# Weights as one stream, all queues ordered by a timeline simulation, and the first block's waits moved, in a two-layer hybrid decoder trunk

## The chip, the cores and the metric

The kernel runs on one core of a Trainium2 chip. The metric is the device time of one execution in microseconds (us). A core has five engines that run side by side, each with its own queue of instructions in a fixed order: TensorE (PE, matmuls; its weight loads are shown apart as PEld), VectorE (DVE), ScalarE (ACT), GpSimd (POOL) and SyncE (SP), which here only issues DMA transfers. An engine takes its instructions strictly in their order, and each of them waits until what it reads is written and what it overwrites has been read.

## What is computed

The reference is a trunk of `DEPTH` = 2 layers over one sequence of 512 tokens and 1024 channels, in float32. Cut to what matters:

```python
for l in range(DEPTH):
    u = rmsnorm(h, norm_w[l])
    proj = u @ w_in[l]                       # one combined input projection
    ret_p, diff_p, ssd_p, ml_p = split_cols(proj, ...)
    ret_out  = retention_mixer(...) * silu(rz)          # chunks of 128 tokens, a state carried over
    diff_out = diff_attention_mixer(...) * silu(dz)     # softmax(q1 k1) - lam * softmax(q2 k2), causal
    ssd_out  = _rms(ssd_mixer(...) * silu(sz)) * ssd_norm_w[l]   # Mamba-2, causal conv, chunked scan
    ml_out   = mlstm_mixer(...) * silu(mz)              # stabilised mLSTM, causal conv, chunked
    mix = concatenate([ret_out, diff_out, ssd_out, ml_out])      # 2048 wide
    h = h + mix @ w_out[l]
return rmsnorm(h, final_norm_w)
```

## The kernel before, in words

**Precision and tiles.** Each matmul operand is split into a high part and a low part, and each product takes three matmuls: high by high, low by high, high by low. A matmul row in the trace is mostly 128x128 weights against 128x512 data. The input projection has 15 blocks of 512 columns per layer, each 8 slices (`k`) of 128 input channels deep; the output projection has four groups (`r`, `d`, `s`, `m`, one per mixer) of two halves with 4 slices each. The list `ORDER` names the sequence of a layer: mLSTM's blocks first (`mv`, `gates`, `mq`, ...), then those of differential attention, then `m` (the out-projection of mLSTM), the blocks of SSD, `d`, and so on to `r`, which ends the layer. `proj_tok` runs a block with tokens on the output's partitions, `proj_feat` one with features there, `out_proj` an out-projection, which adds its result onto the residual `h` (L657).

**Weights.** `split_w` loads two slices (512 KB) with one DMA on SP's queue (L366) into one of 2 buffers named `raw`; `split_half` then makes for each slice `whi` on ACT (a cast, L357, or L360 with a scale for out-projections) and `wlo` on DVE (a subtraction, L358, or L361 with the scale). There are 10 buffers of `whi` and 10 of `wlo`, so one block of 8 slices and 2 slices of the next fit. A `raw` buffer comes free when both `wlo` made of it are done. `load_block` and `out_proj` issue the 4 loads of a block in the program where its projection begins. The first block of all (`mv` of layer 0) has its weights loaded by `start` in 8 pieces named `z`.

**What sets the order.** TensorE's order is written by a planner in the kernel: the projections form a main line (`filler`), and the mixers are generators that are put into it (`spawn`, `later`, `due`, `drive`) at times which the planner counts by costs in the table `W`. ACT, DVE, POOL and SP are ordered by the framework's scheduler from the program's order and its priorities: in the kernel before by priority, with the splits of weights raised by `high_priority(W["hp"])`, 100. The first block (`start`) is under `manual_schedule` for ACT, DVE, POOL and SP: there the written order counts.

**The first block.** `start` has steps per token tile `t`: `squares(t)` (ACT, L390), `scale(t)` (two small DVE instructions L395 and L397, then a power -0.5 on POOL, L240), `mul(t)` (two DVE instructions L404 that write the normed tile `e`), `trans(t)` (8 transposes on PE, L131, in two banks, then a copy `uh` on ACT, L347, and a subtraction `ul` on DVE, L348). `hi(k)` and `lo(k)` make `whi` and `wlo` of slice `k` (L414, L418). `run(pr[t], n)` lets the projection of tile `t` issue n of its 16 pieces; the string `orders` lists the pieces (`h3` is the two matmuls with `whi` of slice 3, `l3` the one with `wlo`). `setup` also issues matmuls of a tile of ones (`warm`). The small parameter loads (`rows`, `w`, `cv`) are prepared by ACT (L313) and DVE (L304, L314, L295, L298).

**Places that are named later.** L1157 is a DVE copy of a PSUM bank in `diff_av` (differential attention); L544 multiplies a gate into the bank of a projection; L954 is a product in `ssd` that TensorE's next matmuls read; L950 and L995 stand ahead of it; L604 and L606 apply rotary embeddings; L623 makes the low part of a mixer's output for `out_proj`; L253, L257, L260, L240 and L330 are the norm of the next layer (squares on ACT, two small DVE steps, the power on POOL, the product on DVE).

Of the kernel before, what the change touches and what calls it, by code (L numbers as in the profile page):

```python
# [11 lines left out]
F32 = mybir.dt.float32  # L12
# [9 lines left out]
NT = S // P  # L22
# [41 lines left out]
     'sN': 0.0, 'sF': 7.3, 'rC': 2.3, 'rN': 3.0, 'dT': 9.14, 'dN': 1.0, 'dM': 3.0, 'dV': 6.68, 'dF': 14.0,  # L64
     'm0': 6.4, 's0': 8.8, 'dT1': 0.6, 'dN1': 1.0, 'hp': 100, 'he': 100, 'hr': 50, 'hd': 50, 'dS': 4.7, 'dQ': 6.0,
     'ha': 50}
# [33 lines left out]
class Trunk:  # L100
    def __init__(self, ctx, tc, aps, dbg=None):
        self.tc, self.nc = tc, tc.nc
        self.x, self.win, self.wg, self.wout, self.nrm, self.rows, self.convp, self.cst, self.out = aps
        self.dbg = dbg or {}
        mk = lambda n, b, **k: ctx.enter_context(tc.tile_pool(name=n, bufs=b, **k))
        self.cp = mk("cp", 1)


        self.small = mk("small", 1)
        self.hp = mk("hp", 1)  # L110
        self.pool = mk("pool", 1)
# [87 lines left out]
    def setup(self):  # L199
# [151 lines left out]
    def split_half(self, raw, scale):  # L351
        nc = self.nc
        hi = self.t("whi", [P, 512], F32R, bufs=10)
        lo = self.t("wlo", [P, 512], F32R, bufs=10)
        with self.tc.high_priority(W["hp"]):
            if scale is None:
                nc.scalar.copy(out=hi, in_=raw)  # L357
                nc.vector.tensor_tensor(out=lo, in0=raw, in1=hi.bitcast(F32), op=ALU.subtract)  # L358
            else:
                nc.scalar.activation(hi, raw, AF.Copy, scale=scale)  # L360
                nc.vector.scalar_tensor_tensor(lo, raw, scale, hi.bitcast(F32), ALU.mult, ALU.subtract)  # L361
        return hi, lo
# [5 lines left out]

    def load_block(self, name):
        b = BIDX[name]  # L370
        return [q for g in range(4) for q in self.split_w(self.win[self.l, b, :, 2 * g:2 * g + 2, :])]

    def start(self, evac):
# [46 lines left out]
        with self.tc.manual_schedule(engines={E.Activation, E.DVE, E.Pool, E.SP}):  # L420
# [206 lines left out]
    def out_proj(self, g, mixt, tok_outer=False, after=None, cut=False, heads=False):  # L627
        nc = self.nc
        gi = GROUPS[g]
        nw = self.nwc[g]  # L630
        w = [[x for q in range(2) for x in self.split_w(self.wout[self.l, gi, half, :, 2 * q:2 * q + 2, :],
                                                        nw[2 * q:2 * q + 2])]
             for half in range(2)]
        l = self.l
        order = [(t, hf) for t in range(NT) for hf in range(2)] if tok_outer else \
                [(t, hf) for hf in range(2) for t in range(NT)]
        for t, hf in order:
# [5 lines left out]
            for c0, c1 in zip(cuts, cuts[1:]):  # L643
# [5 lines left out]
                for k in range(4):  # L649
                    hi, lo = w[hf][k]  # L650
# [705 lines left out]
```

## Time and profile before

| | |
|---|---|
| median of 3 runs | 1045.69 us (1043.56 to 1046.55) |
| the profiled execution | 1043.91 us, of which the span from first to last instruction is 1042.1 us |
| mean granted TensorE clock | 0.994 |
| PE busy | 1023.0 us (98% of the span), 5110 instructions |
| DVE / ACT / POOL busy | 693.2 us (67%) / 479.7 us (46%) / 164.9 us (16%) |
| DMA | 93.84 MB, mean 90 GB/s; the weights' loads of 512 KB land 3.9 us (w_in) and 3.5 us (w_out) after they are issued |

A row of the trace's timeline has the start, the duration, the engine, the line, the operation with out<-in, the shape and a count; in brackets stands the idle time of the engine before it and what released it. Idle time counts only on the engine that sets the end.

### The profile page before, as it was taken

The numbers are of one execution on the slowest core, as the hardware profiler recorded it, in microseconds if no ns is written. First come the engines' busy times: TensorE is split into PE (matmuls) and PEld (weight loads), VectorE is DVE, ScalarE is ACT, GpSimd is POOL, SyncE is SP. The second block draws the span as 40 slices with busy tenths as digits, with TensorE's granted clock in tenths as the row PEclk, the third lists the DMA queues.
The fourth block names the chain that finished last, engine by engine and source line by source line (L and its number), as shares of the span: only waits on it lengthen the run. The fifth ranks groups of instructions, "written<-read, shape, count | busy, mean of one in ns | idle before, by whom it ended". The sixth has DMA issues, their size and how long they took to land.

```text
span 1042.1 us, 14190 instructions
## 1 busy us (share of the span) xinstructions
PE 1023.0 (98%) x5110; PEld 835.1 (80%) x5110; DVE 693.2 (67%) x1495; ACT 479.7 (46%) x1057; POOL 164.9 (16%) x204
## 2 busy tenths in 40 slices
PE   8999999999999999999999999999999999999997
PEld 6788888877778887878887888887777888878786
DVE  5588675567787867446655967666667786863454
ACT  4444336545455444433343542575444553553332
POOL 2000132101111233022000012210001112510301
PEclk9999999999999999999999999999999999999999
DMA  7324322322212413313122422233121233233112
GB/s 254 107 72 122 102 71 82 101 82 81 79 44 85 128 51 102 102 61 126 41 84 80 138 85 81 82 101 103 60 86 56 81 100 103 81 102 101 42 60 81
DMA packets 39144, 93.84 MB, mean 90 GB/s; under 512 B 3849, under 2 KB 16777, under 8 KB 38946
## 3 DMA queue, kind: packets, MB, share of 16 engines
q1 hardware_dynamic: 38064, 91.49, 28.7%
q10 hardware_dynamic: 1010, 1.45, 0.4%
q8 instruction: 40, 0.66, 0.3%
q14 instruction: 30, 0.25, 0.1%
HBM read 90.78 MB, written 2.15 MB: 89 GB/s over the span
## 4 chain that ended last, share of the span: by engine, by line
PE 90%; DVE 5%; issue 1%; ACT 1%; DMA 1%; POOL 0%; POOLq 0%; DVEq 0%; ACTq 0%
PE pspj L127 74%; PE psS L127 6%; PE psacc L127 6%; PE psS L131 4%; DMA raw<-in_w_in_dram 1%; DVE wlo L361 1%; DVE w L950 1%; DVE ft L606 0%; DVE z L1291 0%; DVE wlo L358 0%; DVE h L657 0%; DVE z L544 0%; ACT e L253 0%; DMA raw<-in_w_out_dram 0%; DVE wlo L418 0%
## 5 line engine op out<-in xcount | busy, mean ns | idle before, releaser
L358 DVE TENSOR_TENSOR wlo<-raw,whi 128x512 fp32r<-128x512 f32 x248 | 174.0, 721 | 67.4 <-ACT whi L357 61.8
L127 PE MATMUL pspj<-whi,uh 128*128 128x512 f32 x512 | 209.7, 410 | 0.0
L127 PE MATMUL pspj<-whi,ul 128*128 128x512 f32 x512 | 200.9, 392 | 0.0
L127 PE MATMUL pspj<-wlo,uh 128*128 128x512 f32 x512 | 197.7, 393 | 2.4 <-DVE wlo L418 2.2
L357 ACT CAST whi<-raw 128x512 fp32r<-128x512 f32 x248 | 147.8, 618 | 108.5 <-PE pspj L127 60.8
L127 PE MATMUL pspj<-uh,whi 128*128 128x512 f32 x448 | 179.2, 400 | 0.0
L127 PE MATMUL pspj<-uh,wlo 128*128 128x512 f32 x448 | 174.7, 390 | 0.0
L127 PE MATMUL pspj<-ul,whi 128*128 128x512 f32 x448 | 174.6, 390 | 0.0
L127 PEld LDWEIGHTS pspj<-wlo,uh 128*128 128x128 f32 x512 | 96.5, 189 | 25.1 <-DVE wlo L418 3.9
L127 PEld LDWEIGHTS pspj<-whi,uh 128*128 128x128 f32 x512 | 97.0, 189 | 22.4 <-issue 3.0
L127 PEld LDWEIGHTS pspj<-whi,ul 128*128 128x128 f32 x512 | 96.9, 189 | 17.8 <-DVE ul L348 0.4
L127 PE MATMUL pspj<-whi,mh 128*128 128x512 f32 (+1 forms) x260 | 105.2, 405 | 4.3 <-DVE w L1157 4.3
L240 POOL TENSOR_TENSOR s<-s,nhalf 128x4 f32<-128x4 f32 (+1 forms) x44 | 35.8, 813 | 417.5 <-DVE s L1181 122.9
L127 PE MATMUL pspj<-whi,ml 128*128 128x512 f32 (+1 forms) x260 | 101.4, 390 | 0.3
L127 PE MATMUL pspj<-wlo,mh 128*128 128x512 f32 (+1 forms) x260 | 101.2, 389 | 0.0
L127 PEld LDWEIGHTS pspj<-uh,wlo 128*128 128x128 f32 x448 | 84.1, 188 | 18.2
L127 PEld LDWEIGHTS pspj<-uh,whi 128*128 128x128 f32 x448 | 84.2, 188 | 17.4 <-issue 0.7
L127 PEld LDWEIGHTS pspj<-ul,whi 128*128 128x128 f32 x448 | 84.3, 188 | 16.0
L584 DVE SCALAR_TENSOR_TENSOR e<-pspj,cvh,e 128x511 f32<-128x511 f32 (+2 forms) x90 | 67.0, 744 | 9.6 <-ACT e L582 8.4
L602 ACT ACTIVATE e<-pspj 32x512 f32<-32x512 f32 x96 | 56.6, 589 | 20.0 <-PE pspj L127 18.7
L657 DVE TENSOR_TENSOR h<-pspj,h 128x512 f32<-128x512 f32 (+1 forms) x65 | 43.6, 678 | 28.7 <-PE pspj L127 28.3
L127 PEld LDWEIGHTS pspj<-whi,mh 128*128 128x128 f32 x260 | 49.3, 190 | 15.4 <-DVE w L1157 5.2
(221 smaller groups left out, 1406.4 us busy)
## 6 DMA issues: line engine op xcount, KB each, us to landing
raw<-in_w_in_dram SPq DMA_DIRECT2D x116, 512.0 KB, 3.9
raw<-in_w_out_dram SPq DMA_DIRECT2D x32, 512.0 KB, 3.5
bcm<-adr SPq DMA_DIRECT2D x16, 256.0 KB, 3.3
z<-in_w_in_dram SPq DMA_DIRECT2D x8, 256.0 KB, 6.6
bcm<-gdr SPq DMA_DIRECT2D x8, 256.0 KB, 3.8
out_dram<-z SPq DMA_DIRECT2D x7, 256.0 KB, 2.0
h<-in_x_dram SPq DMA_DIRECT2D x3, 512.0 KB, 6.5
cst<-in_consts_dram SPq DMA_DIRECT2D x1, 1035.0 KB
```

The costliest lines, as they stand in the source:

```text
L127: self.nc.tensor.matmul(out, lhsT=lhsT, rhs=rhs, start=start, stop=stop, **kw)
L131: self.nc.tensor.transpose(out, src, self.ident if ident is None else ident)
L240: self.nc.gpsimd.tensor_tensor(out=out, in0=m, in1=self.nhalf[:, :n], op=ALU.pow)
L357: nc.scalar.copy(out=hi, in_=raw)
L358: nc.vector.tensor_tensor(out=lo, in0=raw, in1=hi.bitcast(F32), op=ALU.subtract)
L361: nc.vector.scalar_tensor_tensor(lo, raw, scale, hi.bitcast(F32), ALU.mult, ALU.subtract)
L584: nc.vector.scalar_tensor_tensor(acc[:, s:], p[:, 0:S - s], w[:, 3 - s:4 - s], acc[:, s:], ALU.mult, ALU.add)
L602: nc.scalar.activation(x[q * 32:q * 32 + 32, :], p[o * 32:o * 32 + 32, :], AF.Copy, scale=scale)
L657: nc.vector.tensor_tensor(out=hs, in0=p, in1=hs, op=ALU.add)
L950: nc.vector.scalar_tensor_tensor(e[:, j * P:(j + 1) * P], ab[g][:, j, :], self.ncs[:, t, h:h + 1], self.cap, ALU.add, ALU.min)
```

## The change

Four things are changed.

1. The weights of all blocks come from one generator, `stream`, in the order of `ORDER`. `feed` advances it by one DMA and its two splits. The projections call `feed` when the last use of a pair of slices has been issued (last tile, odd `k`), `start` calls it once after `gates_w`, and `piece` calls it where a slice is asked for that has not been issued.
2. `high_priority` around the splits is gone, and the framework orders all queues by a simulated timeline (`schedule_with_timeline_sim=True`).
3. `warm(3)`, three matmuls of the tile of ones behind the broadcast of the norm's weights, is gone.
4. In the first block the steps and the pieces stand in another order: `l4` and `l6` stay on POOL but come after `trans(1)`, `l7` goes from POOL to DVE, `trans(1)` comes before `l4 l6 l3`, and the later tiles take all `h` before all `l`.

```diff
@@ setup @@
-        warm(3)
@@ split_half @@
-        with self.tc.high_priority(W["hp"]):
-            if scale is None:
-                nc.scalar.copy(out=hi, in_=raw)
...
+        if scale is None:
+            nc.scalar.copy(out=hi, in_=raw)
...
-    def load_block(self, name):
-        b = BIDX[name]
-        return [q for g in range(4) for q in self.split_w(self.win[self.l, b, :, 2 * g:2 * g + 2, :])]
+    def stream(self, depth):
+        for l in range(depth):
+            for name in ORDER:
+                if (l, name) == (0, "mv"):
+                    continue
+                if name in BIDX:
+                    for g in range(4):
+                        yield (l, name), self.split_w(self.win[l, BIDX[name], :, 2 * g:2 * g + 2, :])
+                elif name in GROUPS:
+                    for half in range(2):
+                        for q in range(2):
+                            yield (l, name), self.split_w(
+                                self.wout[l, GROUPS[name], half, :, 2 * q:2 * q + 2, :],
+                                self.nwc[name][2 * q:2 * q + 2])
+    def feed(self):
+        for key, pieces in self.weights:
+            self.wts.setdefault(key, []).extend(pieces)
+            return
+    def piece(self, key, k):
+        while len(self.wts.get(key, ())) <= k:
+            self.feed()
+        return self.wts[key][k]
@@ start @@
-            orders = ["h0 h1 l0 l1 h2 h3 h4 h6 l2 h5 l4 l3 h7 l6 l5 l7", "h0 h1 h2 h3 l0 l1 l2 l3 h4 h5 h6 h7 l4 l5 l6 l7"]
+            orders = ["h0 h1 l0 l1 h2 h3 h4 h6 l2 h5 h7 l4 l6 l3 l5 l7", "h0 h1 h2 h3 h4 h5 h6 h7 l0 l1 l2 l3 l4 l5 l6 l7"]
...
             hi(6, nc.vector.tensor_copy)
-            lo(4, nc.gpsimd)
             scale(1)
             lo(2)
             hi(5)
             hi(7)
             mul(1)
+            run(pr[0], 5)
+            trans(1)
+            lo(4, nc.gpsimd)
             lo(6, nc.gpsimd)
             lo(3)
-            run(pr[0], 6)
-            trans(1)
+            run(pr[1], 4)
             lo(5)
-            lo(7, nc.gpsimd)
-            run(pr[0], 2)
+            lo(7)
+            run(pr[0], 3)
             squares(2)
...
             self.gates_w()
+            self.feed()
             run(pr[2], 8)
@@ proj_tok (proj_feat and out_proj alike) @@
-        w = w or self.load_block(name)
...
+        get = (lambda k: w[k]) if w else (lambda k: self.piece(key, k))
...
+            if t == NT - 1 and k % 2 and 1 in parts:
+                self.feed()
@@ the module's end @@
-    with tile.TileContext(nc) as tc:
+    with tile.TileContext(nc, schedule_with_timeline_sim=True) as tc:
```

Line numbers after the change are some 30 higher: L404 becomes L427, L414 L437, L418 L441, L131 L133, L240 L241, L544 L575, L657 L685, L1157 L1185, L954 L982, L330 L331, L348 L349; L357, L358, L360, L361 and L366 stay.

TensorE's order is the same before and after from the end of the first block on; the first 135 rows differ, and three matmuls of ones are missing. SP issues the same loads in nearly the same order: in each layer one weight load stands about ten places from where it stood, and one broadcast of SSD's decays (`bcm<-adr`) comes ahead of one or two weight loads. Of DVE's 1375 rows about 270 pieces stand elsewhere, most by a place or two; of ACT's 115 pieces, of POOL's five.

**POOL and PE in the first block.** `s` is the norm's scale, `wlo` a low part, `psS` a bank of transposes (the first matmuls below write `psS` from the normed tile `e`), `pspj_174` and `pspj_251` (after: `pspj_171`, `pspj_236`) the banks of tile 0 and tile 1. POOL before:

```order
L240 TENSOR_TENSOR s_23_142<-s_22_140,nhalf 128x1
L418 TENSOR_TENSOR wlo_194<-z_116,whi_190 128x512
L240 TENSOR_TENSOR s_43_200<-s_42_198,nhalf 128x1
L418 TENSOR_TENSOR wlo_212<-z_120,whi_192 128x512
L418 TENSOR_TENSOR wlo_241<-z_122,whi_206 128x512
L566 MEMSET v_262 128x4
L240 TENSOR_TENSOR s_62_269<-s_61_267,nhalf 128x1
```

POOL after:

```order
L241 TENSOR_TENSOR s_23_139<-s_22_137,nhalf 128x1
L241 TENSOR_TENSOR s_42_195<-s_41_193,nhalf 128x1
L441 TENSOR_TENSOR wlo_230<-z_113,whi_187 128x512
L441 TENSOR_TENSOR wlo_232<-z_117,whi_189 128x512
L597 MEMSET v_267 128x4
L241 TENSOR_TENSOR s_62_274<-s_61_272,nhalf 128x1
```

The power for tile 1 (the second L240) no longer stands behind a `wlo`, and one `wlo` has left POOL. PE before, from the last pieces of tile 0 ahead of `trans(1)`:

```order
L127 MATMUL pspj_174<-wlo_202,uh_75 128x512
L127 MATMUL pspj_174<-whi_204,uh_75 128x512
L127 MATMUL pspj_174<-whi_204,ul_76 128x512
L127 MATMUL pspj_174<-wlo_194,uh_75 128x512
L127 MATMUL pspj_174<-wlo_214,uh_75 128x512
L131 MATMUL psS_225<-cst,e_208 128x128 x4
L131 MATMUL psS_232<-cst,e_209 128x128 x4
L127 MATMUL pspj_174<-whi_206,uh_75 128x512
L127 MATMUL pspj_174<-whi_206,ul_76 128x512
L127 MATMUL pspj_174<-wlo_212,uh_75 128x512
L127 MATMUL pspj_251<-whi_148,uh_75 128x512
L127 MATMUL pspj_251<-whi_148,ul_76 128x512
```

PE after, at the same place:

```order
L129 MATMUL pspj_171<-wlo_197,uh_75 128x512
L129 MATMUL pspj_171<-whi_199,uh_75 128x512
L129 MATMUL pspj_171<-whi_199,ul_76 128x512
L129 MATMUL pspj_171<-whi_201,uh_75 128x512
L129 MATMUL pspj_171<-whi_201,ul_76 128x512
L133 MATMUL psS_216<-cst,e_203 128x128 x4
L133 MATMUL psS_223<-cst,e_204 128x128 x4
L129 MATMUL pspj_236<-whi_145,uh_75 128x512
L129 MATMUL pspj_236<-whi_145,ul_76 128x512
L129 MATMUL pspj_236<-whi_163,uh_75 128x512
L129 MATMUL pspj_236<-whi_163,ul_76 128x512
L129 MATMUL pspj_236<-whi_165,uh_75 128x512
```

Two of the three `wlo` matmuls that stood ahead of the transposes (`wlo_194`, `wlo_214`) are now behind them; `h7` (two matmuls with `whi_201`) stands ahead in their place, so that 19 projection matmuls of tile 0 come before `trans(1)` either way. Ahead of the next transposes (tile 2) PE has 17 matmuls before the change and 25 after it.

**DVE at 249 us (and, in the same order of lines, at 757 us in layer 1).** `w_2424<-psS_2422` (after: `w_2441<-psS_2439`) is the copy that frees a PSUM bank of differential attention. Before:

```order
L361 SCALAR_TENSOR_TENSOR wlo_2485<-raw_2478,cv_131,whi_2484 128x512
L361 SCALAR_TENSOR_TENSOR wlo_2491<-raw_2488,cv_131,whi_2490 128x512
L361 SCALAR_TENSOR_TENSOR wlo_2495<-raw_2488,cv_131,whi_2494 128x512
L1184 TENSOR_TENSOR s_696_2378<-s_696_2378,s_694_2372 128x4
L544 SCALAR_TENSOR_TENSOR z_2431<-e_2429,pspj_2264 128x512
L1186 TENSOR_TENSOR w_2381<-psacc_2014,s_696_2378 128x512
L544 SCALAR_TENSOR_TENSOR z_2456<-e_2454,pspj_2385 128x512
L1157 COPY w_2424<-psS_2422 128x128
L1138 RECIPROCAL s_708_2415<-rsum_2275 128x1
```

After:

```order
L575 SCALAR_TENSOR_TENSOR z_2448<-e_2446,pspj_2271 128x512
L1212 TENSOR_TENSOR s_701_2385<-s_701_2385,s_699_2379 128x4
L361 SCALAR_TENSOR_TENSOR wlo_2460<-raw_2453,cv_128,whi_2459 128x512
L361 SCALAR_TENSOR_TENSOR wlo_2478<-raw_2475,cv_128,whi_2477 128x512
L1214 TENSOR_TENSOR w_2388<-psacc_2021,s_701_2385 128x512
L1185 COPY w_2441<-psS_2439 128x128
L361 SCALAR_TENSOR_TENSOR wlo_2482<-raw_2475,cv_128,whi_2481 128x512
L1166 RECIPROCAL s_718_2432<-rsum_2282 128x1
L575 SCALAR_TENSOR_TENSOR z_2503<-e_2501,pspj_2392 128x512
```

The copy (L1157, now L1185) has one `wlo` and one L544 fewer ahead of it; both stand behind it now.

**DVE between the layers, at 520 to 532 us.** `h_82` is the residual of tile 3, `e` the normed tile that is transposed next, `raw_5054` and `raw_5064` (after: `raw_5001`, `raw_5032`) two pairs of slices of layer 1's first block. Before:

```order
L358 TENSOR_TENSOR wlo_5057<-raw_5054,whi_5056 128x512
L257 TENSOR_SCALAR s_1783_4979<-s_1781_4976 128x1
L358 TENSOR_TENSOR wlo_5061<-raw_5054,whi_5060 128x512
L358 TENSOR_TENSOR wlo_5067<-raw_5064,whi_5066 128x512
L358 TENSOR_TENSOR wlo_5071<-raw_5064,whi_5070 128x512
L260 TENSOR_SCALAR s_1785_4983<-s_1781_4976,s_1783_4979 128x1
L657 TENSOR_TENSOR h_82<-pspj_4972,h_82 128x512
L330 SCALAR_TENSOR_TENSOR e_4987<-h_81,s_1786_4985,bcm_4860 128x512
L330 SCALAR_TENSOR_TENSOR e_4989<-h_81,s_1786_4985,bcm_4861 128x512
L306 TENSOR_REDUCE s_1793_4999<-w_4997 128x2
L348 TENSOR_TENSOR ul_4871<-psS_5023,uh_4870 128x4x128
```

After:

```order
L307 TENSOR_REDUCE s_1803_5016<-w_5014 128x2
L358 TENSOR_TENSOR wlo_5004<-raw_5001,whi_5003 128x512
L685 TENSOR_TENSOR h_82<-pspj_4979,h_82 128x512
L331 SCALAR_TENSOR_TENSOR e_4994<-h_81,s_1791_4992,bcm_4867 128x512
L331 SCALAR_TENSOR_TENSOR e_4996<-h_81,s_1791_4992,bcm_4868 128x512
L358 TENSOR_TENSOR wlo_5008<-raw_5001,whi_5007 128x512
L358 TENSOR_TENSOR wlo_5035<-raw_5032,whi_5034 128x512
L358 TENSOR_TENSOR wlo_5039<-raw_5032,whi_5038 128x512
L311 TENSOR_TENSOR nlam_5020<-s_1804_5018 128x1
L349 TENSOR_TENSOR ul_4878<-psS_5060,uh_4877 128x4x128
L258 TENSOR_SCALAR s_1831_5098<-s_1829_5095 128x1
L685 TENSOR_TENSOR h_82<-pspj_5043,h_82 128x512
```

Three of the four `wlo` now stand behind the residual's sum (L657, now L685) and the two products L330 (now L331). Further down, the pair of L331 for tile 3 stands between the two `wlo` of the next pair (after: `wlo_5053` and `wlo_5057`), where before both `wlo` (5077 and 5081) stood ahead of it.

In the SSD section of each layer (at 404 and 913 us) one more `wlo` (L358) stands ahead of the two L954 than before, and in the out-projection at 338 and 847 us L623 has moved ahead of a product of the causal convolution (L589).

More of the change, by code (lines that the diff above doesn't have):

```diff
@@ L64 @@
      'sN': 0.0, 'sF': 7.3, 'rC': 2.3, 'rN': 3.0, 'dT': 9.14, 'dN': 1.0, 'dM': 3.0, 'dV': 6.68, 'dF': 14.0,
-     'm0': 6.4, 's0': 8.8, 'dT1': 0.6, 'dN1': 1.0, 'hp': 100, 'he': 100, 'hr': 50, 'hd': 50, 'dS': 4.7, 'dQ': 6.0,
+     'm0': 6.4, 's0': 8.8, 'dT1': 0.6, 'dN1': 1.0, 'he': 100, 'hr': 50, 'hd': 50, 'dS': 4.7, 'dQ': 6.0,
      'ha': 50}
@@ L113, in __init__ @@
         self.ps = mk("ps", 1, space=bass.MemoryType.PSUM)
+        self.weights = self.stream(DEPTH)
+        self.wts = {}
         self.banks = [(0.0, b) for b in range(8)]
@@ L354, in split_half @@
         lo = self.t("wlo", [P, 512], F32R, bufs=10)
-        with self.tc.high_priority(W["hp"]):
-            if scale is None:
[L357 to L361, printed above, removed]
+        if scale is None:
+            nc.scalar.copy(out=hi, in_=raw)
+            nc.vector.tensor_tensor(out=lo, in0=raw, in1=hi.bitcast(F32), op=ALU.subtract)
+        else:
+            nc.scalar.activation(hi, raw, AF.Copy, scale=scale)
+            nc.vector.scalar_tensor_tensor(lo, raw, scale, hi.bitcast(F32), ALU.mult, ALU.subtract)
         return hi, lo
@@ L498, in proj_tok @@
     def proj_tok(self, name, evac, w=None, toks=range(NT), order=None):
-        w = w or self.load_block(name)
+        toks = list(toks)
+        key = self.l, name
+        get = (lambda k: w[k]) if w else (lambda k: self.piece(key, k))
         steps = [(t, k, parts) for t in toks for k, parts in order] if order else \
-                [(t, k, (0, 1)) for t, k in self.steps_of(list(toks), name != "mv")]
+                [(t, k, (0, 1)) for t, k in self.steps_of(toks, name != "mv")]
         banks, n = {}, {}
@@ L512, in proj_tok @@
                     n[t] += 1
-                    self.mm(p, lhsT=u[:, k, ts_], rhs=w[k][part], start=(n[t] == 1), stop=(n[t] == 3 * KD))
+                    self.mm(p, lhsT=u[:, k, ts_], rhs=get(k)[part], start=(n[t] == 1), stop=(n[t] == 3 * KD))
+            if t == NT - 1 and k % 2 and 1 in parts:
+                self.feed()
             yield
@@ L520, in proj_feat @@
     def proj_feat(self, name, evac):
-        w = self.load_block(name)
+        key = self.l, name
         banks = {}
@@ L525, in proj_feat @@
             fs = slice(f * P, (f + 1) * P)
-            hi, lo = w[k][0][:, fs], w[k][1][:, fs]
+            hi, lo = [x[:, fs] for x in self.piece(key, k)]
             self.mm(p, lhsT=hi, rhs=self.uh[:, k, :], start=(k == 0), stop=False)
@@ L529, in proj_feat @@
             self.mm(p, lhsT=lo, rhs=self.uh[:, k, :], start=False, stop=(k == KD - 1))
+            if f == 3 and k % 2:
+                self.feed()
             yield
@@ L628, in out_proj @@
         nc = self.nc
[L629 to L633, printed above, removed]
         l = self.l
@@ L649, in out_proj @@
                 for k in range(4):
-                    hi, lo = w[hf][k]
+                    hi, lo = self.piece((l, g), 4 * hf + k)
                     mh, ml = m(t, k)
@@ L654, in out_proj @@
                     self.mm(p, lhsT=mh, rhs=lo[:, cs], start=False, stop=(k == 3))
+                    if t == NT - 1 and k % 2 and c1 % 512 == 0:
+                        self.feed()
                     yield
```

## The prediction, made before the changed kernel had run

> **What bounds the kernel now.** I read the chain of waits first, then what TensorE waited for, then the timeline around each of those waits. The first two rows are the page's shares of the chain and one of its pieces, a steady stretch:
>
> ```profile
> PE 90%; DVE 5%; issue 1%; ACT 1%; DMA 1%; POOL 0%; POOLq 0%; DVEq 0%; ACTq 0%
> ```
>
> ```profile
> 161.81 44.93 PE pspj L127 x198
> ```
>
> TensorE sets the end: 198 matmuls in 44.93 us are 0.227 us each, and these the change leaves as they are. So it can win only what PE waits for (total us, times, longest):
>
> ```profile
> PE pspj L127 <- DVE w L1157: 4.3, 2, 2.2
> PE psacc L127 <- DVE w L954: 3.1, 2, 1.6
> PE pspj L127 <- DVE wlo L418: 2.2, 1, 2.2
> ```
>
> 9.6 us in five waits, all on DVE. To that comes the granted clock. Stretches with PEclk in the column after the five engines' busy times:
>
> ```profile
> 247.00:253.00 6.00, 3.87 (x18) 2.82 (x17) 5.85 (x12) 4.63 (x10) 1.71 (x4) 1.00 0.53 173
> 757.00:760.00 3.00, 0.80 (x3) 0.58 (x3) 2.93 (x9) 2.61 (x7) 1.39 (x4) 0.87 0.78 225
> 760.00:764.00 4.00, 4.00 (x15) 3.23 (x14) 2.51 (x4) 0.72 (x2) 0.31 (x1) 0.67 0.42 125
> 915.00:920.00 5.00, 5.00 (x24) 4.31 (x24) 3.45 (x8) 1.25 (x3) 0.56 (x1) 0.66 0.51 170
> 403.00:408.00 5.00, 3.52 (x24) 2.97 (x24) 4.95 (x9) 1.85 (x4) 0.00 (x0) 1.00 0.39 117
> ```
>
> After the wait at 757 PE lacks 3.0 x 0.13 + 4.0 x 0.33 = 1.7 us of full clock, after that at 913 5.0 x 0.34 = 1.7; after the wait at 403, of nearly the same length as that at 913, nothing. So a wait of about 1.7 us stands at the edge of costing 1.7 more, and the one of 2.2 us for L1157 did so at 757 and not at 249.
>
> **The first block.** POOL, DVE and PE before, one view each:
>
> ```profile
> 13.08 1.42 POOL L418 TENSOR_TENSOR wlo<-z,whi 128x512 fp32r<-128x512 f32 x1 [6.96 <-DVE whi L414]
> 14.45 1.01 POOL L240 TENSOR_TENSOR s<-s,nhalf 128x1 f32<-128x1 f32 x1
> ...
> 23.45 0.55 POOL L240 TENSOR_TENSOR s<-s,nhalf 128x1 f32<-128x1 f32 x1 [5.48 <-DVE s L397]
> ```
>
> ```profile
> 13.57 0.21 DVE L397 TENSOR_SCALAR s<-s,s 128x1 f32<-128x1 f32 x1 [0.16 <-ACT e L390]
> 13.70 1.35 DVE L418 TENSOR_TENSOR wlo<-z,whi 128x512 fp32r<-128x512 f32 x1
> 15.49 1.40 DVE L404 SCALAR_TENSOR_TENSOR e<-h,s,psS 128x512 f32<-128x512 f32 x2 [0.45 <-POOL s L240]
> 16.82 1.66 DVE L418 TENSOR_TENSOR wlo<-z,whi 128x512 fp32r<-128x512 f32 x1
> ```
>
> ```profile
> 18.53 0.80 PE L127 MATMUL pspj<-wlo,uh 128*128 128x512 f32 x1 [2.24 <-DVE wlo L418]
> 19.12 1.91 PE L131 MATMUL psS<-cst,e 128*128 128x128 f32 x8
> ...
> 25.24 1.03 PE L131 MATMUL psS<-cst,e 128*128 128x128 f32 x8
> ```
>
> Tile 1's power waits on POOL behind a `wlo`, tile 1's `e` behind that, and then PE waits 2.24 us for the DVE `wlo` ahead of the transposes. After the change the power starts behind L397, at 13.8, and takes about 0.55, its duration at 23.45, instead of 1.01. The DVE `wlo` at 13.70, without POOL beside it, takes about 0.64 (529.00: 1.28 for two), so `e` runs from 14.4 to 15.8 and the transposes from 15.9 to about 16.9 instead of 19.12 to 21.03, with the same 19 matmuls ahead: 4.1 us earlier. `wlo` of slice 7, which goes to DVE, stands behind the copies of the transposes, where DVE waits for ACT anyway. Part is given back. Tile 2's `e` now has L305, L296 and L299 ahead of it, which want the parameter loads:
>
> ```profile
> L288 SPq DMA_DIRECT2D cv<-in_conv_dram x2: 328/328/328, 11.7 to 14.8; - x2
> ...
> DMA to landing us min/median/max: 9.7/9.7/9.7
> ```
>
> `cv` lands at 11.75 + 9.7 = 21.45. Then 0.6 for three small DVE steps, 0.55 for the power, 1.4 for `e`, 0.5 for the second half's transposes and some 0.1 between each: tile 2's transposes end near 24.6 instead of 26.27, 1.67 earlier and with 8 more matmuls behind them (25 instead of 17), 8 x 0.227 = 1.8. Together -3.4 (I round down for the wait for tile 1's `uh` and `ul`). Ends: -4.1 if nothing is given back, -1.5 if the 8 matmuls are not done by then. [...]
>
> [...]
>
> **The copy at 249 and 757.** DVE before, then PE, in layer 0:
>
> ```profile
> 247.71 1.41 DVE L361 SCALAR_TENSOR_TENSOR wlo<-raw,cv,whi 128x512 fp32r<-128x512 f32 x2
> ...
> 250.31 0.68 DVE L544 SCALAR_TENSOR_TENSOR z<-e,pspj 128x512 f32<-128x512 f32 x1
> 250.91 0.29 DVE L1157 COPY w<-psS 128x128 f32<-128x128 f32 x1
> ```
>
> ```profile
> 248.73 0.39 PE L127 MATMUL pspj<-wlo,uh 128*128 128x512 f32 x1
> 251.25 0.50 PE L127 MATMUL pspj<-whi,mh 128*128 128x512 f32 x1 [2.13 <-DVE w L1157]
> ```
>
> PE's first matmul of group `m` needs the bank that the copy reads. One `wlo` (1.41 / 2, 0.66 from start to start) and one L544 (0.60) leave its front, and what it reads is there by 249.1, since PE stops then: it ends 1.26 us earlier, in both layers, and PE waits 0.9 instead of 2.1. That is -2.5. The `wlo` and L544 behind it hold nobody up: the next rows of DVE serve PE several us later. [...]
>
> **The products at 404 and 913.** PE waits 1.49 here, and L954 gets one more `wlo` ahead of it, 0.60 from start to start; L950 comes earlier by the L995 that moves behind, to no use:
>
> ```profile
> 404.93 0.52 PE L127 MATMUL psacc<-w,w 128*128 128x64 f32 x3 [1.49 <-DVE w L954]
> ```
>
> +0.6 in each layer, +1.2; and at 404 a wait of 2.1 brings the 1.7 of half clock with about even odds: +0.9. (At 913 it is paid already.)
>
> **The boundary of the layers.** A `raw` load before, its cast, PE's use of slice 7's `wlo`, and DVE:
>
> ```profile
> 521.85 0.33 SPq L366 DMA_DIRECT2D raw<-in_w_in_dram  x1
> ```
>
> ```profile
> 525.74 1.14 ACT L357 CAST whi<-raw 128x512 fp32r<-128x512 f32 x2 [1.31 <-DMA raw<-in_w_in_dram]
> ```
>
> ```profile
> 531.07 0.39 PE L127 MATMUL pspj<-wlo,uh 128*128 128x512 f32 x1
> ```
>
> ```profile
> 529.00 1.28 DVE L358 TENSOR_TENSOR wlo<-raw,whi 128x512 fp32r<-128x512 f32 x2
> 530.20 0.20 DVE L260 TENSOR_SCALAR s<-s,s 128x1 f32<-128x1 f32 x1
> 531.07 1.41 DVE L330 SCALAR_TENSOR_TENSOR e<-h,s,bcm 128x512 f32<-128x512 f32 x2 [0.66 <-POOL s L240]
> ```
>
> The pair for slices 6 and 7 is loaded when the `wlo` of slice 3 has freed its buffer. That `wlo` moves behind a residual sum and two products, so the issue slides from 521.85 to about 524.9, the landing to 528.8 (3.9 later), the casts to 530.0, and slice 6's `wlo` just fits (530.2, wanted three matmuls before 531.07, at 530.4). Slice 7's stands behind the next two products (1.4) and ends near 532.2; PE read it at 531.07: +1.1, once. Ends: 0, if the products come early, and +2.4, if the residual sum waits for PE as before.
>
> **Small pieces.** L623 moves ahead of L589 in both layers; those who waited for it:
>
> ```profile
>   PEld pspj L127: 1.1, 2
> ```
>
> Of 1.1 us one matmul each (0.23) is covered, the rest goes: -0.6. At 142 and 650 (L846) a cast moves ahead of an exponential on ACT, which idles there: 0, at worst a cast's 0.57 each (525.74: 1.14 for two). SP's shifted loads and POOL's rest: the buffers of ten slices run ahead of PE by several us, so 0; without that cover a pair that is late costs what it is late.
>
> **Sum.** -3.4 - 2.5 - 1.7 - 0.6 + 1.2 + 0.9 + 1.1 = -5.0 on the profiled 1043.91: 1038.9. The median of the runs is 1.78 above that execution, so 1040.7. A difference of 0.3% (3.1 us) is about what a measurement of this kernel can tell.
>
> **Rivals.**
> - The gain is eaten. The start gives 1.5, the half clock at 757 stays or appears at 404, and 531 costs 2.4: -1.5 - 2.5 - 0.6 + 1.2 + 1.7 + 2.4 = +0.7, about 1046. For it: the waits at 404 and 531 grow; against it: the 2.24 at 18.53 and 1.26 at each copy have their cause taken away by the order itself, whatever the loads do.
> - The stream does nothing by itself: SP's order of loads is almost the same, so loads come no earlier. I think that likely; then the time is set by the terms above, and alone the DVE order and the start count. It does not change the forecast.
> - Slower, by loads that come late. DVE and ACT take things strictly in order, and without priority a `wlo` may stand behind an instruction that waits, as at 531. A delayed `wlo` delays the next load, which takes 3.9 + 0.6 + 0.7 = 5.2 us to reach PE. If at two more places per layer DVE delays a `wlo` by over about 2.6 us, each costs some 1.1 and a half clock of 1.7: 4 x 2.8 = +11.2, about 1052. For it: 270 pieces of DVE's order moved; against it: most by one or two places, 0.6 to 1.4 us, less than the slack.
> - More is won: no half clock at all (another -1.7 at 913, none at 404) and the start at -4.1: about 1037.
>
> [...]
>
> **Chances.** Forecast with its neighbours (1038 to 1042.5) 0.48, more won 0.18, gain eaten 0.20, slower 0.14. Faster by over 0.3% (below 1042.5) 0.66, within 0.3% 0.19, slower 0.15. The range of 8 in 10 is 1035 to 1048.
>
> **What would show it.** `trans(1)` on PE ending near 17 and no wait for L441; the wait for L1185 at 0.9 to 1.0 each, full clock at 757; that for L982 at 2.1 each; a new wait of about 1 us for `wlo` L358 at 531. I am wrong if PE waits for `whi` or `wlo` at places where it did not, or if its waits sum to more than the 9.6 us of before.

## The result and the profile after

The changed kernel takes 1049.73 us (median of 9 runs, 1048.06 to 1055.13) against 1043.91 us (9 runs, 1039.93 to 1046.55) of the kernel before in the same comparison: 1.006 times as long, 95% interval 1.004 to 1.008. It is slower by 0.6%, where 1040.7 was forecast, and lies above the range.

The profiled execution is the slowest of the nine (1055.13, 5.4 above the median; span 1053.2). Its chain of waits has less of PE than before:

```profile
PE 82%; DVE 8%; DMA 5%; issue 2%; ACT 2%; POOL 1%; SPq 0%; POOLq 0%; ACTq 0%; DVEq 0%
```

What PE waited for after the change (total us, times, longest):

```profile
PE psS L129 <- DVE ft L620: 6.1, 2, 3.2
PE psacc L129 <- DVE w L982: 3.3, 2, 1.8
PE pspj L129 <- DVE w L1185: 1.7, 2, 0.9
PE psS L129 <- ACT w L713: 1.1, 1, 1.1
```

The copy L1185 went as forecast, and the first block nearly so. At the top stands a wait that was not there: the causal convolution's result `ft` (L620, before L589), 3.2 us in layer 0 and 3.0 in layer 1. The second newcomer is L713, the copy of the mLSTM gates. In this execution each wait of 1.1 us or more is followed by a stretch of lower clock (PEclk is the third column from the end):

```profile
48.00:52.00 4.00, 4.00 (x12) 3.11 (x12) 2.87 (x14) 0.00 (x0) 0.00 (x0) 0.60 0.18 71
100.00:104.00 4.00, 2.96 (x13) 2.48 (x14) 1.98 (x3) 0.86 (x2) 0.00 (x0) 0.80 0.37 123
104.00:108.00 4.00, 4.00 (x20) 3.42 (x19) 1.62 (x4) 1.42 (x6) 1.26 (x3) 0.77 0.00 0
408.00:412.00 4.00, 3.35 (x18) 3.29 (x19) 3.12 (x7) 0.72 (x2) 0.00 (x0) 0.70 0.47 136
412.00:416.00 4.00, 4.00 (x10) 3.06 (x10) 1.54 (x4) 0.72 (x1) 1.84 (x2) 0.50 0.00 0
770.00:774.00 4.00, 3.28 (x16) 2.72 (x17) 3.21 (x8) 1.96 (x6) 2.74 (x4) 1.00 0.70 199
```

The last row is the place that had the low clock before (there 757 to 764), now at full clock.

Since PE's order is the same behind the first block, the start of the same matmul in both traces gives how far one execution lies behind the other. The steps of that distance, in us (each is a difference of two starts; plus is later after the change):

| place (us in before) | wait itself | clock behind it | forecast |
|---|---|---|---|
| first block, to 39.7 | -3.0 | | -3.4 |
| gates at 47 (L713) | +1.2 | +1.6 | 0 |
| `ft` at 98 (L620) | +3.3 | +1.6 | 0 |
| copy at 251 | -1.3 | | -1.25 |
| products at 405 (L982) | +0.1 | +3.2 | +0.6, +0.9 |
| boundary at 531 | +0.6 | | +1.1 |
| `ft` at 606 | +3.0 | +1.6 | 0 |
| copy at 759 | -1.3 | -1.4 | -1.25, -1.7 |
| products at 915 | +0.2 | +1.6 | +0.6 |
| L874 (127, 635), L623 | +0.1 | | -0.6 |

The waits sum to +2.9, the clock to +8.2; together 11.1 of the 11.2 us between the two profiled executions. (The -3.0 of the first row holds 1.7 us of low clock that stood there before and is gone.) The medians lie 5.8 apart, so a run at the median pays some 5 us less of low clock than this one. The granted clocks of the nine runs agree: 0.988 here, which is 12.6 us of the span, and 0.992 to 0.994, some 8 to 6 us, in seven of the other eight.

**Where `ft` loses 3.2 us.** DVE after the change, then SP, in layer 0:

```profile
73.77 0.68 DVE L358 TENSOR_TENSOR wlo<-raw,whi 128x512 fp32r<-128x512 f32 x1
76.78 0.88 DVE L867 SCALAR_TENSOR_TENSOR w<-bcm,g,cap 128x128 f32<-128x128 f32 x3 [2.33 <-DMA bcm<-gdr]
77.57 0.75 DVE L615 SCALAR_TENSOR_TENSOR e<-pspj,cvh,e 128x510 f32<-128x510 f32 x1
...
93.49 0.69 DVE L358 TENSOR_TENSOR wlo<-raw,whi 128x512 fp32r<-128x512 f32 x1 [1.26 <-ACT whi L357]
...
100.29 0.69 DVE L620 SCALAR_TENSOR_TENSOR ft<-e,e 128x512 f32<-128x512 f32 x1 [0.76 <-ACT e L618]
```

```profile
72.69 0.38 SPq L841 DMA_DIRECT2D bcm<-gdr  x1
```

And PE, which needs the last `ft`:

```profile
101.04 0.49 PE L129 MATMUL psS<-ft,ft 128*128 128x128 f32 x2 [3.17 <-DVE ft L620]
```

L867 (before L839) adds mLSTM's gates to `bcm`, a broadcast of them from DRAM, which SP issues at 72.69 and which lands 4.1 us later. DVE comes to it at 74.45 and stands still for 2.33 us. The remaining steps of the convolution (L615), which need nothing of `bcm`, are queued behind it. Before the change the same instruction stood behind the steps on `mt` and `g`, and found its data there; the second row is the last `ft`, which PE takes next:

```profile
78.74 0.35 DVE L839 SCALAR_TENSOR_TENSOR w<-bcm,g,cap 128x128 f32<-128x128 f32 x1
...
97.18 0.69 DVE L589 SCALAR_TENSOR_TENSOR ft<-e,e 128x512 f32<-128x512 f32 x1 [0.76 <-ACT e L587]
```

Before, `ft` was ready at 97.87 (97.18 + 0.69) and PE started on it at 97.93: 0.06 us was to spare, so whatever DVE lost ahead of it PE lost too. What remains beside the 2.33 us is at 93.49, a `wlo` that waits for the cast of a load which came late. The chain of waits shows its way: DVE makes a `wlo`, this frees `raw`, the next load takes 3.88 us, is cast, and the `wlo` of it holds up the convolution. In layer 1 the same two standstills are 2.16 us (L867) and 1.20 us (`wlo`). The chain:

```profile
88.26 0.61 DVE wlo L358
...
88.89 3.88 DMA raw<-in_w_in_dram
...
92.84 0.63 ACT whi L357
...
94.10 0.75 DVE e L615
```

### The profile page after: what moved, and what is told of

The parts are those of the page before. It is cut to its first block, busy times and chain, and to the rows that moved or that the text cites. A ratio compares the mean times of both kernels' runs of the same rounds, so it can differ in the third digit from the quotient of the medians.

```text
span 1053.2 us, 14173 instructions
## 1 busy us (share of the span) xinstructions
PE 1030.2 (98%) x5104; PEld 838.3 (80%) x5104; DVE 698.2 (66%) x1496; ACT 480.0 (46%) x1057; POOL 171.3 (16%) x203
## 4 chain that ended last, share of the span: by engine, by line
PE 82%; DVE 8%; DMA 5%; issue 2%; ACT 2%; POOL 1%; SPq 0%; POOLq 0%; ACTq 0%; DVEq 0%
PE pspj L129 68%; PE psacc L129 6%; PE psS L129 5%; PE psS L133 3%; DMA raw<-in_w_in_dram 3%; DVE wlo L358 1%; DVE e L615 1%; DMA w<-in_rows_dram 1%; DVE w L867 1%; DVE w L978 1%; DMA z<-in_w_in_dram 1%; ACT whi L357 1%; POOL s L241 0%; ACT e L254 0%; DVE h L685 0%
## 5 line engine op out<-in xcount | busy, mean ns | idle before, releaser
L358 DVE TENSOR_TENSOR wlo<-raw,whi 128x512 fp32r<-128x512 f32 x248 | 173.7, 715 | 70.9 <-ACT whi L357 67.1
L357 ACT CAST whi<-raw 128x512 fp32r<-128x512 f32 x248 | 147.6, 619 | 122.2 <-PE pspj L129 60.4
L241 POOL TENSOR_TENSOR s<-s,nhalf 128x4 f32<-128x4 f32 (+1 forms) x44 | 39.2, 891 | 418.8 <-DVE s L1209 204.9
L615 DVE SCALAR_TENSOR_TENSOR e<-pspj,cvh,e 128x511 f32<-128x511 f32 (+2 forms) x90 | 66.9, 744 | 10.6 <-ACT e L613 9.9
L685 DVE TENSOR_TENSOR h<-pspj,h 128x512 f32<-128x512 f32 (+1 forms) x65 | 43.8, 677 | 24.8 <-PE pspj L129 24.5
```

The lines of the kernel that those rows point to most:

```text
L241: self.nc.gpsimd.tensor_tensor(out=out, in0=m, in1=self.nhalf[:, :n], op=ALU.pow)
L615: nc.vector.scalar_tensor_tensor(acc[:, s:], p[:, 0:S - s], w[:, 3 - s:4 - s], acc[:, s:], ALU.mult, ALU.add)
L685: nc.vector.tensor_tensor(out=hs, in0=p, in1=hs, op=ALU.add)
```

## The experiments

The intervals are ratios to the kernel before, run on the same chip (its medians were 1043.85, 1043.73 and 1044.82 us in the three groups).

**`L867` held behind `ft` (pin_w).** The changed kernel with an edge in DVE's order, which waits for nothing: in each layer the four L867 of the first chunk come behind the `ft` that was late because of them.

```diff
-            nc.vector.scalar_tensor_tensor(o, th, 1.0, acc, ALU.add, ALU.mult)
+            self.convs.append(nc.vector.scalar_tensor_tensor(o, th, 1.0, acc, ALU.add, ALU.mult))
...
+                if t == 0:
+                    self.tc.add_manual_dep(x.ins, self.convs[-5].ins.name, mybir.DependencyInfo(
+                        mybir.DependencyClass.NoSync, mybir.DependencyReason.DATA), reason="late")
```

> The changed kernel with one ordering edge per layer: the four products w<-bcm of mLSTM's first chunk (L867 in the changed kernel) are issued on DVE behind the convolution product ft (L620) that they stood ahead of; PE's and POOL's orders stay, on ACT the exponential of w moves behind one convolution step. Theory A: in the changed kernel the first of these products waits 2.33 us for its broadcast from DRAM, everything behind it on DVE and the exponential's followers on ACT are late by that and more, and PE pays 3.3 + 3.0 us at 101 and 617 us plus up to 1.7 of half clock each. Then PE's wait for L620 is gone, and the time is 6 to 9 us under the changed kernel's 1049.7: 1041 to 1044. Rival B: the convolution chain is late because the splits of weights lost their priority and DVE is full there; then the wait for L620 stays above 2 us in both layers and the time stays within 2 us of 1049.7.

Measured: 1041.93 us (12 runs, 1039.28 to 1047.39), 0.9988 (0.9969 to 1.0008); 7.8 less than the changed kernel. DVE at the place, and PE's waits:

```profile
77.61 0.69 DVE L621 SCALAR_TENSOR_TENSOR ft<-e,e 128x512 f32<-128x512 f32 x1 [0.50 <-ACT e L619]
78.22 1.14 DVE L868 SCALAR_TENSOR_TENSOR w<-bcm,g,cap 128x128 f32<-128x128 f32 x4
...
91.01 0.69 DVE L359 TENSOR_TENSOR wlo<-raw,whi 128x512 fp32r<-128x512 f32 x1 [1.14 <-ACT whi L358]
```

```profile
PE psacc L130 <- DVE w L986: 3.5, 2, 1.8
PE pspj L130 <- DVE w L1189: 1.7, 2, 0.9
PE psS L130 <- DVE ft L621: 1.2, 2, 0.7
```

`ft` came 3.45 us earlier (81.06 to 77.61), PE's wait for the last `ft` fell from 6.1 to 1.2, and the low clock behind it is gone in this profile: 4.9 + 3.2 = 8.1 against 7.8 measured. This sum is no proof by itself, since the two profiled executions lie 14.1 us apart: pin_w's has full clock behind the products L986 too, where PE waits no less than after the change (3.5 in all). The granted clocks of all runs bear it out. A run's time less what the clock took of its span (span x (1 - granted clock), good to half a us) has a median of 1042.1 after the change, 1038.1 in pin_w and 1038.0 in the kernel before: 4.0 us less in pin_w, near the 4.9 of the waits. The clock took 8.0 us of a run after the change on average, 4.7 in pin_w and 5.8 before: 3.3 less in pin_w, near the 3.2.

So the place of these products costs what was read, shown by taking it away, and it is the largest of the steps in the table. The 1.2 left is, as the trace reads, the late `wlo` at 91.01 and its like in layer 1. And the kernel is still no faster than before, though the copies have won what was forecast: more was lost elsewhere.

**The parts alone.** First the new first block alone, with `warm(3)` gone (start_only):

```diff
-        warm(3)
-            orders = ["h0 h1 l0 l1 h2 h3 h4 h6 l2 h5 l4 l3 h7 l6 l5 l7", ...]
+            orders = ["h0 h1 l0 l1 h2 h3 h4 h6 l2 h5 h7 l4 l6 l3 l5 l7", ...]
...
```

> The kernel before with only the first block's part of the change: warm(3) gone, the new order of steps and pieces; priorities, scheduler and loads as before. Theory A: the projections of the first block are done 3.0 us earlier, but about 1.2 us go back at the gates (45 us), since ACT copies their bank behind casts that wait for loads which come no earlier, and a half clock may follow: 1 to 2 us less than before, 1042 to 1043 against 1043.9, hardly to be told apart. Rival C, the term as it was predicted: 3.4 us less, 1040.5.

Measured: 1043.26 us (12 runs, 1039.41 to 1045.95), 0.9991 (0.9974 to 1.0009): no difference. The loss at the gates that I expected did not come; the gain itself is smaller. PE is ahead by only 1.1 us at 39.7, where the changed kernel was by 3.0. Between 24 and 28 us ACT has no gap, and PE is busy for 2.97 only; in the whole run it waits 0.5 us each for `uh` and `ul`, which are made of the transposes. After the change ACT is busy for 1.84 there. Start_only, then the changed kernel:

```profile
24.00:28.00 4.00, 2.97 (x15) 1.84 (x15) 3.16 (x8) 4.00 (x10) 0.00 (x0) 1.00 0.19 41
```

```profile
24.00:28.00 4.00, 3.97 (x22) 3.20 (x21) 2.92 (x9) 1.84 (x4) 1.17 (x6) 1.00 0.06 16
```

Next, the simulated timeline alone on the kernel before (sim_only); the splits' priority stays in the program.

```diff
-    with tile.TileContext(nc) as tc:
+    with tile.TileContext(nc, schedule_with_timeline_sim=True) as tc:
```

> The kernel before with only the scheduling by a simulated timeline; loads per block, priorities of the splits and first block as before. On DVE and ACT its order is that of the changed kernel but for the first block and a few rows. Theory A: all waits that were new at 101, 409, 538 and 617 us appear here, and the gains at 255 and 771 too: 6 to 8 us more than before, 1050 to 1052, with PE waiting about 3 us for the convolution's ft (L589) in both layers. Rival D: the stream of weights (loads issued at other places) makes the difference; then this one is within 1.5 us of the kernel before.

Measured: 1054.08 us (6 runs, 1052.22 to 1055.61), 1.0093 (1.0066 to 1.012): slower by 10.2, 2 us beyond what I expected. The late `ft` comes with this flag alone:

```profile
78.57 0.88 DVE L839 SCALAR_TENSOR_TENSOR w<-bcm,g,cap 128x128 f32<-128x128 f32 x3 [2.17 <-DMA bcm<-gdr]
```

```profile
PE psS L127 <- DVE ft L589: 6.2, 2, 3.2
```

Last, the changed kernel without the flag (sim_off): the stream, no priority, the new first block.

```diff
-    with tile.TileContext(nc, schedule_with_timeline_sim=True) as tc:
+    with tile.TileContext(nc) as tc:
```

> The changed kernel without the scheduling by a simulated timeline: stream, splits without priority, and the new first block stay. DVE has the first of the products w<-bcm at nearly the same place as the changed kernel here, the other three later. Theory A: only that one product can wait for its broadcast, and what it holds up is less: a wait of 0 to 2 us at PE for L620, and the waits at 249 and 759 us as before (2.1 each): 1042 to 1047. Rival B (priority of the splits): splits come late in many places, and PE shows several new waits for whi or wlo, 1048 or more.

Measured: 1033.16 us (6 runs, 1032.39 to 1033.52), 0.9894 (0.9871 to 0.9917). That is far below what I expected (1042 to 1047): the change without its flag is faster by 1.1%, and the flag costs 16.6 us on top of it. Nothing waits for the copies at 249 and 757, nor for `ft`:

```profile
PE psacc L129 <- DVE w L982: 1.6, 2, 0.8
PE psS L133 <- ACT w L1041: 1.5, 2, 0.9
```

L867 stands ahead of the convolution here too, but the gates are through sooner and its broadcast is issued at 65.22 instead of 72.69, so DVE waits for it only 0.47 us (SP, then DVE):

```profile
65.22 0.39 SPq L841 DMA_DIRECT2D bcm<-gdr  x1
```

```profile
69.50 0.35 DVE L867 SCALAR_TENSOR_TENSOR w<-bcm,g,cap 128x128 f32<-128x128 f32 x1 [0.47 <-DMA bcm<-gdr]
```

So a place ahead of the convolution is not the fault by itself; it is right only if the transfer comes in time.

**What won in sim_off: the priority.** The kernel before without `high_priority` around the splits, nothing else (no_hp):

```diff
-        with self.tc.high_priority(W["hp"]):
-            if scale is None:
-                nc.scalar.copy(out=hi, in_=raw)
...
+        if scale is None:
+            nc.scalar.copy(out=hi, in_=raw)
...
```

> The kernel before without the priority of the splits (100) and with nothing else changed: loads per block, old first block, ordinary scheduling. Theory E: the priority is what put wlo ahead of the bank copy at 249 and 759 us and of the products at 404 and 914 us; without it PE no longer waits at the first two (-2.3 each) and 0.7 less at each of the others, and the half clock behind them goes (-1.7 to -3.4): -6 to -9 us, 1035 to 1038. Rival F: only with the stream are splits traced late enough; here they are traced where a block begins, so that program order alone puts them early and the waits stay: within 2 us of 1043.9.

Measured: 1031.85 us (4 runs, 1030.99 to 1032.33), 0.9888 (0.9871 to 0.9906). One line taken away wins 11.9 us, more than expected. PE's largest wait (1.0, 0.7 and 0.4 are left), then DVE and PE at the copy:

```profile
PE pspj L127 <- DVE wlo L417: 2.2, 1, 2.2
```

```profile
247.97 0.28 DVE L1156 COPY w<-psS 128x128 f32<-128x128 f32 x1
```

```profile
249.19 0.40 PE L127 MATMUL pspj<-whi,mh 128*128 128x512 f32 x1
```

The copy is done 0.9 us before PE wants its bank. Both copies (-2.3 and -2.4) and both pairs of products (-1.6 and -1.8) lose their whole wait, and with them goes the low clock at 757 and 913: what PE waited for at these four places stood behind `wlo` that the priority had put ahead of it. At the products the loss is again a standstill. In the kernel before a pair of `wlo` waits 1.72 us for its casts, which wait for a load, and L606 and L978, which need nothing of it, are queued behind; in no_hp these two come first.

```profile
394.36 1.29 DVE L358 TENSOR_TENSOR wlo<-raw,whi 128x512 fp32r<-128x512 f32 x2 [1.72 <-ACT whi L357]
```

The reverse, sim_off with the priority put back (hp_back):

```diff
+        with self.tc.high_priority(100):
```

> The run sim_off (stream, new first block, ordinary scheduling) with the priority 100 of the splits put back. Theory E: the waits at 249 and 759 us (2.1 each) and the longer ones at 404 and 914 come back with their half clocks: +6 to +9 on 1033.2, so 1039 to 1042. Rival F: the stream itself issues the splits where they hold nobody up; then it stays within 2 us of 1033.2. Against the run start_only (1043.3), which differs from it by the stream alone, Theory E says at most 2.5 us, from the start, where the stream left PE 2.5 us earlier at 39 us.

Measured: 1048.24 us (6 runs, 1047.38 to 1053.17), 1.0054 (1.0034 to 1.0074), 15.1 above sim_off and 6 above the 1039 to 1042 that I expected. The waits for L983 (5.2 in all) and the copy L1186 (4.1) are back, and a new one for the gates (2.9 in two; layer 0):

```profile
71.89 0.30 PE L133 MATMUL psS<-cst,w 96*128 96x96 f32 x1 [1.54 <-DVE w L803]
```

With the priority the stream costs 5.0 (1048.24 against start_only's 1043.26), where I expected at most 2.5; without it, less (below).

**Two further versions, faster than both kernels.** In sim_off, SSD's gate and norm (L1041) raised by a priority of 60 (best):

```diff
+        with self.tc.high_priority(60):
             nc.vector.tensor_tensor(out=yd, in0=yd, in1=zs[t], op=ALU.mult)
...
-            "sz": tok("sz", self.ev_silu(sz, "z", 8)),
+            "sz": tok("sz", self.ev_silu(sz, "z", 8, 60)),
```

> The run sim_off with a priority of 60 on the gate of SSD's output (tanh on ACT and L575 on DVE) and on the norm behind it. On DVE the gate's product and L1031 of the first tile come ahead of one or two wlo, on ACT two rows move by three places; all else is the same. In sim_off PE waited 0.8 and 1.1 us at 424 and 930 us for L1041 at the end of this chain. If the chain's place behind the wlo is the cause, both waits go: 1.3 to 1.9 us less than 1033.2, 1031.4 to 1032.0, and the waits for wlo do not grow. If another link (POOL's power, the transposes' bank) sets it, the time is within 0.5 of 1033.2.

Measured: 1030.68 us (4 runs, 1030.52 to 1031.63), 0.988 (0.9859 to 0.9901), 2.5 below sim_off, somewhat more than expected; the waits for L1041 (1.5) are gone. The intervals of the two ratios overlap, but the slowest run here (1031.63) is below the fastest of sim_off (1032.39).

And no_hp with the new first block of start_only; no stream and no simulated timeline (no_hp_start):

```diff
-        with self.tc.high_priority(W["hp"]):
...
-        warm(3)
...
-            lo(4, nc.gpsimd)
...
+            run(pr[0], 5)
+            trans(1)
+            lo(4, nc.gpsimd)
...
```

> The kernel before with two parts: the splits without priority (as in no_hp, 1031.85) and the new first block with warm(3) gone (as in start_only). No stream, ordinary scheduling. Theory G: with nothing late at the gates the start's gain stays: PE about 1 to 3 us earlier at 39 us and later, and the half clock at 16 to 24 us goes (-1.7): 1028 to 1031. Rival: as in start_only the gain is gone by 60 us, because the loads of the next blocks land at the same time: 1031 to 1032.5, the same as no_hp.

Measured: 1029.81 us (5 runs, 1029.59 to 1030.66), 0.9854 (0.9834 to 0.9875): the fastest, though its interval overlaps those of best and no_hp. PE is 1.9 us ahead at 39.7 and some 1.5 us ahead of no_hp to the end, and the `wlo` wait that no_hp still had is gone. What is left of waits above 0.5 in all:

```profile
PE psS L127 <- DVE ones L213: 1.0, 1, 1.0
PE psS L127 <- DVE ft L588: 0.8, 2, 0.5
PE psacc L127 <- DVE w L845: 0.7, 2, 0.3
```

## Why the prediction was wrong, point by point

- **The step that failed** is the cover of everything that moved and was not one of the named places: "against it: most by one or two places, 0.6 to 1.4 us, less than the slack", and for SP and POOL's rest 0. It measured a move in durations of what is passed, and not by what the moved instruction waits for. L867's move put an instruction that waits for a transfer ahead of ones that don't: 2.33 us of standstill. And there was next to no slack, since `ft` came to PE with 0.06 us to spare. By pin_w it cost 7.8 us with its clock. Forecast was -5.0 and measured +5.8, so this is the larger part of the 10.8 between them. The sign that I had named came with it: PE's four largest waits after the change sum to 12.2 us, more than the 9.6 of before.
- **The rival "slower"** named the right kind, an in-order DVE behind an instruction that waits, and the right price of the clock for one place (1.7; measured 1.6), but a third of that of the wait (1.1; measured 3.2). It looked for weight loads and PE's wait for a `wlo`; the larger part was the broadcast, the smaller (the `wlo` at 93.49) its own chain, and PE waited for `ft` both times. I gave it 0.14.
- **Copies at 249 and 757:** right: -1.3 each, wait 0.9, and full clock at 757 (-1.4 against -1.7 forecast). For the -1.7 of the sum, the low clock at 757, no run shows a rule by which a wait of 0.9 leaves the clock full; what the runs showed is that after the change the wait was 0.86 us at both copies and PEclk stayed at 1.00 behind it (254 to 262 and 770 to 778), and that in no_hp, with no wait there, it is 1.00 from 752 to 760.
- **First block:** right in size, -3.0 against -3.4. The rows after:

```profile
13.25 0.93 POOL L241 TENSOR_TENSOR s<-s,nhalf 128x1 f32<-128x1 f32 x1 [7.28 <-DVE s L420]
```

```profile
15.09 1.24 PE L133 MATMUL psS<-cst,e 128*128 128x128 f32 x8
...
23.75 1.28 PE L133 MATMUL psS<-cst,e 128*128 128x128 f32 x8 [0.92 <-DVE e L427]
```

  The power took 0.93 and not 0.55, beside the `wlo` that DVE began meanwhile. The transposes ended at 16.3 (forecast 16.9), those of tile 2 at 25.0 (24.6). Part of the gain I had not named, though a difference of starts holds it: before, low clock went with the wait at 18.53 (16 to 24 us, 4.0 x 0.18 + 4.0 x 0.25 = 1.7), and after the change it is gone. By start_only this order wins 1.1 at 39.7 with the old scheduling, and by no_hp_start 1.9, so the -3.0 leans on the rest of the change, and that the size came out is in part luck. The kernel before:

```profile
16.00:20.00 4.00, 1.76 (x8) 1.29 (x7) 2.48 (x3) 0.00 (x0) 1.97 (x3) 0.82 0.76 283
20.00:24.00 4.00, 4.00 (x17) 3.45 (x16) 2.50 (x7) 2.50 (x7) 0.55 (x1) 0.75 0.34 130
```

- **What I missed behind the first block:** at 45 us PE waits for the copy of the gates, which stands on ACT behind two pairs of casts and the copy of `v` (L598), and the casts wait for loads. It stood behind both pairs before too, and was in time. Now the second pair starts at 43.16, 1.4 earlier than before (44.55), while PE is 3.0 ahead. The changed kernel:

```profile
43.16 1.14 ACT L357 CAST whi<-raw 128x512 fp32r<-128x512 f32 x2 [0.60 <-DMA raw<-in_w_in_dram]
...
44.69 0.57 ACT L713 COPY w<-psS 32x512 f32<-32x512 f32 x1
```

```profile
45.31 1.06 PE L129 MATMUL psS<-cst,w 32*128 32x16 f32 x8 [1.11 <-ACT w L713]
```

  1.2 and a low clock of 1.6 gave nearly all of it back: 0.2 us was left at 60 us. The loads alone don't force this. In sim_off, with the same first block and PE a little further ahead, ACT makes the copy between the two pairs, and PE doesn't wait:

```profile
42.37 0.57 ACT L713 COPY w<-psS 32x512 f32<-32x512 f32 x1
```

- **Products at 404 and 913:** the wait grew by 0.1 and 0.2, not 0.6. L982 stands behind one more `wlo` as said, but the eight products ahead of it (L978, before L950) now begin ahead of the sum L1023 and end at 405.51. The execution is 3.7 behind at this place, so that is 401.8 on the clock of before, where they ended at 402.98: 1.2 earlier. "To no use" was wrong. As the rows read, they would have ended earlier still but for POOL, whose rest I had put at 0. The first four take 4.47 us, each of them beside a row of POOL and done some 0.15 us after it; the last four, with POOL idle, take 0.34 each. Before, three of the eight stood beside POOL so. No run took this away. The low clock at 404, put at even odds for +0.9, came, and with 3.2 us.

```profile
399.99 5.52 DVE L978 SCALAR_TENSOR_TENSOR w<-bcm,g,cap 128x128 f32<-128x128 f32 x8
```

```profile
399.62 1.29 POOL L1008 TENSOR_TENSOR w<-w,w 128x512 f32<-128x512 f32 x1 [4.73 <-DVE w L1006]
...
402.98 1.33 POOL L636 TENSOR_TENSOR e<-e,cst 128x512 f32<-128x512 f32 x1
```

- **Boundary at 531:** the place and mechanism are right (`wlo` L358, 0.42 of wait), the size half: +0.6 for +1.1.
- **Small pieces:** -0.22 and -0.23 at L623's places, against -0.6 in all; the casts put at 0 (L874) cost 0.25 each.
- **The stream does nothing by itself:** half right. sim_off is 3.4 above no_hp_start, which has the same first block and no priority either, so by their medians the stream costs some 3 us with the old scheduling (the ends of their intervals overlap, and they come from different comparisons). The change is several things of opposite sign, and I had priced them by their sum in the order. By medians the priority's removal is worth -11.9, the first block -0.6 (start_only, not clear of noise) to -2.0 (no_hp_start against no_hp), the flag +10.2 alone and +16.6 on top of the rest.

What stays open: why the simulated timeline puts L867 there. That it counts on an earlier landing would fit, but its own times were not measured. Of the 16.6 pin_w explains 7.8; the other 8.8 are, by the steps between pin_w and sim_off in their traces, the start (0.7), the gates at 47 with their clock (2.8), the rest of the `ft` waits, L878 and the boundary (3.1), the copies (2.3) and the products (2.0), less the L1041 that only sim_off has (1.9) and small steps (1.2): 7.8 of the 8.0 between these two profiled executions. They were read, not taken away one by one.

## What to carry to other kernels

Before calling a reordered row harmless, ask what it waits for: an instruction that is moved ahead of a transfer's landing costs the whole standstill, and it costs it to everything queued behind it, down to the next thing that PE takes with no slack. Here that was 2.33 us at one row, 3.2 us at PE and 7.8 us of the kernel. Preparing work (here the splits of weights) should not have the priority over what frees a bank or feeds the bounding engine: taking that priority away alone won 1.1%. A change that bundles a scheduler, a priority and a hand-written order needs each priced by itself, since a gain of 1.1% and a loss of 1.6% showed here as a change of 0.6%.

## What the runs showed of the hardware

- Behind waits of PE of 1.1 us or more the profile after the change shows stretches of low clock that cost 1.6 or 3.2 us: behind 1.11 us (gates) 1.6, behind 3.2 (`ft`) 1.6, behind 1.5 (L982 at 404) 3.2. At 408 to 420 the granted clock lacks 4.0 x 0.30 + 4.0 x 0.50 + 4.0 x 0.06 = 3.4 us; that is twice the 1.7 that the prediction read at 913.

```profile
416.00:420.00 4.00, 4.00 (x20) 3.28 (x19) 1.10 (x3) 0.60 (x1) 0.00 (x0) 0.94 0.02 4
```

  In slices of one us the granted clock there stands at 0.50 from 410 to 416 (0.81 and 0.77 in the slices beside them), and behind the gates at 0.50 from 48 to 51 (0.91 and 0.89 beside them). The slices lack 3.4 and 1.7 us, so by an estimate from them the clock stood at half for twice that, some 6.8 and 3.4 us. The copy's wait of 0.86 us brought none at either place (PEclk 1.00 from 254 to 262 and from 770 to 778), but the 1.54 us for L803 in hp_back (1.00 from 72 to 80), the 1.8 for L986 in pin_w (1.00 from 404 to 420 and from 912 to 928) and the 2.13 at 251 in the kernel before (1.00 from 249 to 261) brought none either: the length of the wait alone does not decide.
- The runs spread with such waits: 1039.63 to 1047.96 for the kernel before in these groups, 1048.06 to 1055.13 after the change, but 1030.99 to 1032.33 (no_hp), 1030.52 to 1031.63 (best) and 1029.59 to 1030.66 (no_hp_start). The versions with at most one wait over 1.0 us are steady to 1.4 us.
- The small DVE products L978 (128x128), 0.34 us each with POOL idle, took 1.07 to 1.37 us beside POOL rows of 1.09 to 1.33 us and ended some 0.15 us after them (at 400 to 404.5 after the change).
